# Five places of a hybrid decoder step: three products given later units, output banks in another order, x blocks requested two ahead

## The chip, the cores and the metric

The kernel runs on one core of a Trainium2 chip. The metric is device time in microseconds, the median of several runs. The three runs of the kernel before took 2066.13, 2067.45 and 2067.91 us: median 2067.45.

## The reference

One inference step of one layer (width 2048, float32). A prompt of 1024 tokens with 16 meta tokens ahead of it, and 8 samples of 4 new tokens each with 1024 past tokens in a paged cache, go through the same layer: RMS norm, one input projection into nine parts, a stick-breaking attention branch (8 heads of 128), a gated linear attention branch (GLA, 4 heads or groups with 128 key and 256 value columns), a SiLU gate on each, one output projection, a second RMS norm and the residual. Shortened to what matters:

```python
def branch_inputs(h, w_in, w_alpha, b_alpha):
    u = h @ w_in
    sq, sk, sv, sg, gq, gk, gv, gg, ga = jnp.split(u, idx, axis=-1)
    log_f = jax.nn.log_sigmoid((ga @ w_alpha + b_alpha).astype(jnp.float32)) / GLA_TAU
    ...
def branch_output(o_sb, sg, o_gla, gg, gla_norm_g, w_out):
    o_gla = rms_norm(o_gla, gla_norm_g)
    mixed = jnp.concatenate([o_sb * jax.nn.silu(sg), o_gla * jax.nn.silu(gg)], axis=-1)
    return mixed @ w_out
def stick_break_weights(z, mask):
    sp = jnp.where(mask, jax.nn.softplus(z), 0.0)
    later = lax.cumsum(sp, axis=z.ndim - 1, reverse=True) - sp
    return jnp.where(mask, jnp.exp(jax.nn.log_sigmoid(z) - later), 0.0)
def gla_chunk(S, q, k, v, g):
    b = jnp.cumsum(g, axis=2)
    decay = jnp.where(causal, jnp.exp(jnp.minimum(b_t - b_s, 0.0)), 0.0)
    attn = jnp.einsum('bhtk,bhsk,bhtsk->bhts', q, k, decay)
    o = attn @ v + (q * jnp.exp(b)) @ S
    S_new = jnp.exp(b_last) * S + (k * jnp.exp(b_last - b)).T @ v
    return S_new, o
def reference(...):
    h = rms_norm(x, norm_pre_g)                     # prompt: 16 meta + 1024 tokens; samples: 8 x 4 tokens
    x = x + rms_norm(branch_output(sb(h), sg, gla(h), gg, gla_norm_g, w_out), norm_post_g)
    # also returned: new keys and values, new GLA states, of the prompt and of the 8 samples
```

## The kernel before

**Products.** TensorE computes everything. A float32 matrix is split into a rounded part and a rest, `h` and `l`, and a product is made of three matmuls (h·h, l·h, h·l; L342 to L344 in the input projection, L1593 to L1595 in the output projection). A split is one cast on ScalarE and one subtraction on VectorE. Input projection: 128 output columns at a time (`inproj`), over 16 blocks of the width, with the 1072 tokens in three pieces that have an accumulator each, `acc` (three PSUM banks).

**Weaving.** Everything else is written as generators, and a `Weaver` puts them between the projection's matmuls: after each unit (6 matmuls of one piece, or 12 of an output step) `beat()` runs the generators that are due. `yield n` means: go on n units later. So the numbers behind `yield` set where in TensorE's order a step stands. A scheduler then orders each engine's instructions by priority; `urgent()` raises it. Each engine runs its own order and waits for others by semaphore. All loads and stores go through SyncE's queue (SP) in its order.

**GLA, per group g (four times).** `inside` makes the key tokens and the packed sample keys: `packed` (L921) transposes a block with three copies of the 32 sample tokens (trp_k, L924), copies it on ScalarE (L925) and subtracts on VectorE (L927), which gives a rounded part and a rest in `pk`. `by_token` and `gv_tok` (L935 to L940) transpose keys and values. All of them use one PSUM buffer with the tag "tr". `chunks` then runs over the prompt in eight chunks (U, L1006, and o, L1010 and L1011) and over the eight samples: `km`, `Us` (L1042), the new state `sn` (L1044); the samples' outputs `os` (L1035) are written four at a time, at b = 0 and b = 5. The samples' old states `Sb` have five buffers; a later one is loaded when an earlier one's new state is made.

**Sample attention.** `new_keys` (L1188) makes the sums over the new keys: the product Cs (L1191), copied to `cn` (L1192), and two units later Cn (L1195). `chain(b)` makes the cumulative sums over one sample's past, C (L1219 to L1222), read by VectorE at L1224. Cs, Cn and C share one PSUM buffer with the tag "C".

**Output projection.** The result is cut into quadrants by an algorithm with seven half-size products p, each in steps (p, q) of 4 token tiles t × 8 weight blocks k. The order is (1,0), (2,0), (1,1), (2,1), (6,0), (6,1), (5,0), (3,0), (5,1), (3,1), (7,0), (4,0), (7,1), (4,1). The four accumulators of a q stay in their banks over its one or two products; `take` reads them after each product (L1443 for p = 1 on ScalarE, L1453, L1456, L1461 and L1464 on VectorE), and TensorE can go on with a bank only after it is read. `bank` (L1427) takes banks in turn from six: numbers 0 to 2 are the input projection's, `acc`, and 3 to 5 those of a pool "m". A weight block is loaded (`wr`, 7 buffers), and split into a `ring` of four places (L1394 ScalarE, L1395 VectorE). `form` (L1340, L1343) makes the stationary side, from parts (q, s) loaded back from DRAM.

**The last steps.** `finish0` (L1509) finishes the first 512 tokens during (7,0) to (4,1): for each of 16 blocks n it loads a block of x (`fetch`, L1518, four buffers), forms the residual sum (L1528) and stores it. `load_keep` loads and splits the last step's weights (L1631 to L1635).

## Time and profile before

| | before |
|---|---|
| median of three runs | 2067.45 us |
| the profiled execution | 2066.38 us |
| its span, first to last instruction | 2064.6 us |
| mean granted TensorE clock | 0.999 |
| TensorE busy | 2024.8 us, 98% |
| VectorE / ScalarE / GpSimd busy | 75% / 46% / 4% |
| mean DMA rate | 146 GB/s |

The timeline gives for each instruction its start, its duration, the engine, the line, the operation with output and inputs, and in brackets how long the engine was idle before it and what released it. An "x3" stands for three in a row. The list of waits sums such idle times by line and releaser. The chain of waits goes back from the last instruction to whatever released each step. In the answer by windows a row has the window and its length, the busy time of TensorE's matmuls, its weight loads, VectorE, ScalarE and GpSimd, then the granted clock, the DMA engines' share and GB/s.

### The profile page before, as it was taken

The page shows a single profiled execution, that of the slowest core. Times are in us where ns is not written, and L with a number is a line of the kernel's source. Part 1 is how long each engine was busy: PE and PEld are TensorE (multiplying, and loading weights), DVE is VectorE, ACT ScalarE, POOL GpSimd, SP SyncE. Part 2 cuts the span into 40 slices and gives each one's busy share as a digit, 9 for nine tenths or more (in the row PEclk, how much of TensorE's full clock was granted, in tenths as well). Part 3 has the DMA queues.
Part 4 walks back from the last instruction along what each step waited for, and adds up shares of the span by engine and source line. Part 5 has one row for each costly group of instructions (what it writes and reads, how often), then busy time and mean ns, then how long its engine had stood idle before and what let it go on. Part 6 is the DMA issues. An engine that isn't in the chain of part 4 may idle for free.

```text
span 2064.6 us, 41985 instructions
## 1 busy us (share of the span) xinstructions
PE 2024.8 (98%) x12507; PEld 1863.6 (90%) x12507; DVE 1552.7 (75%) x6282; ACT 953.4 (46%) x2293; POOL 84.6 (4%) x304
## 2 busy tenths in 40 slices
PE   6999999999999999999999999999999999999998
PEld 5999999999999998999999999998888898788776
DVE  7368989888988989899798897978544347454576
ACT  7355555565655656433534335343433325332332
POOL 0012000101000000000000000000000000000000
PEclk9999999999999999999999999999999999999999
DMA  6354454544455442533433433335776666452485
GB/s 202 103 139 148 139 159 133 171 132 147 146 160 146 140 124 76 139 102 82 108 100 79 125 82 110 98 82 155 236 233 231 220 222 200 139 166 74 129 271 202
DMA packets 371821, 301.85 MB, mean 146 GB/s; under 512 B 42360, under 2 KB 312104, under 8 KB 371592
## 3 DMA queue, kind: packets, MB, share of 16 engines
q1 hardware_dynamic: 371288, 298.64, 48.6%
q8 instruction: 98, 1.61, 0.3%
q14 instruction: 131, 1.07, 0.2%
q10 hardware_dynamic: 304, 0.53, 0.1%
HBM read 241.75 MB, written 57.31 MB: 145 GB/s over the span
## 4 chain that ended last, share of the span: by engine, by line
PE 75%; DVE 12%; DMA 6%; ACT 3%; issue 3%; SPq 0%; POOL 0%; DVEq 0%; ACTq 0%; POOLq 0%
PE acc_g L342 5%; PE acc_g L343 5%; PE acc_g L344 5%; DVE jk L464 5%; PE b L1593 4%; PE b L1595 4%; PE b L1594 4%; PE acc_k L342 3%; PE acc_k L344 3%; PE acc_k L343 3%; PE acc_v L342 2%; PE acc_q L342 2%; PE acc_q L344 2%; PE acc_q L343 2%; PE acc_v L344 2%
## 5 line engine op out<-in xcount | busy, mean ns | idle before, releaser
L464 DVE SCALAR_TENSOR_TENSOR jk<-kp,qb 128x128 f32<-128x128 f32 x2048 | 593.8, 290 | 43.5 <-DMA qb<-qsd 1.7
L342 PE MATMUL acc_g<-hT,wh_g 128*128 128x368 f32 (+2 forms) x768 | 251.4, 327 | 0.5 <-DVE ga L389 0.5
L343 PE MATMUL acc_g<-hT,wh_g 128*128 128x368 f32 (+2 forms) x768 | 247.6, 322 | 0.0
L344 PE MATMUL acc_g<-hT,wl_g 128*128 128x368 f32 (+2 forms) x768 | 247.1, 322 | 0.0
L1593 PE MATMUL b<-ring,f 128*128 128x512 f32 x416 | 164.3, 395 | 3.5 <-ACT gx L521 1.4
L464 DVE DVE_READ_ACCUMULATOR jk<-kp,qb 128x1 f32 x2048 | 167.6, 82 | 0.0
L1594 PE MATMUL b<-ring,f 128*128 128x512 f32 x416 | 162.6, 391 | 0.0
L1595 PE MATMUL b<-ring,f 128*128 128x512 f32 x416 | 162.1, 390 | 0.0
L342 PEld LDWEIGHTS acc_g<-hT,wh_g 128*128 128x128 f32 x768 | 144.5, 188 | 13.3 <-issue 10.8
L343 PEld LDWEIGHTS acc_g<-hT,wh_g 128*128 128x128 f32 x768 | 144.6, 188 | 1.1 <-issue 0.4
L1395 DVE TENSOR_TENSOR ring<-wr,ring 128x512 fp32r<-128x512 f32 x104 | 71.3, 689 | 98.4 <-ACT ring L1394 97.7
L344 PEld LDWEIGHTS acc_g<-hT,wl_g 128*128 128x128 f32 x768 | 144.5, 188 | 0.0
L342 PE MATMUL acc_gv<-hT,wh_gv 128*128 128x400 f32 (+2 forms) x384 | 130.5, 340 | 0.0
L1394 ACT CAST ring<-wr 128x512 fp32r<-128x512 f32 x104 | 64.1, 620 | 139.3 <-PE b L1595 77.0
L342 PE MATMUL acc_k<-hT,wh_k 128*128 128x384 f32 (+1 forms) x384 | 126.4, 329 | 0.0
L343 PE MATMUL acc_gv<-hT,wh_gv 128*128 128x400 f32 (+2 forms) x384 | 125.3, 326 | 0.0
L342 PE MATMUL acc_q<-hT,wh_q 128*128 128x368 f32 (+2 forms) x384 | 125.1, 326 | 0.0
L344 PE MATMUL acc_gv<-hT,wl_gv 128*128 128x400 f32 (+2 forms) x384 | 124.8, 325 | 0.0
L344 PE MATMUL acc_k<-hT,wl_k 128*128 128x384 f32 (+1 forms) x384 | 124.7, 325 | 0.0
L343 PE MATMUL acc_k<-hT,wh_k 128*128 128x384 f32 (+1 forms) x384 | 124.5, 324 | 0.0
L344 PE MATMUL acc_q<-hT,wl_q 128*128 128x368 f32 (+2 forms) x384 | 123.4, 321 | 0.0
L343 PE MATMUL acc_q<-hT,wh_q 128*128 128x368 f32 (+2 forms) x384 | 123.4, 321 | 0.0
(454 smaller groups left out, 5294.3 us busy)
## 6 DMA issues: line engine op xcount, KB each, us to landing
kp<-in_cache_k_dram SPq DMA_DIRECT2D x512, 64.0 KB
vr<-in_cache_v_dram SPq DMA_DIRECT2D x64, 512.0 KB
tf<-in_w_out_dram SPq DMA_DIRECT2D x64, 256.0 KB
td<-tf SPq DMA_DIRECT2D x64, 256.0 KB
qb<-qsd SPq DMA_DIRECT2D x64, 256.0 KB
wr_g<-in_w_in_dram SPq DMA_DIRECT2D x64, 256.0 KB
wr<-td SPq DMA_DIRECT2D x56, 256.0 KB
wr<-in_w_out_dram SPq DMA_DIRECT2D x48, 256.0 KB
```

The lines of the kernel that those rows point to most:

```text
L342: mm(acc[c][:, :n], wh, hh[k][:, lo:hi], start=(k == 0), stop=False)
L343: mm(acc[c][:, :n], wh, hl[k][:, lo:hi], start=False, stop=False)
L344: W.mark = mm(acc[c][:, :n], wl, hh[k][:, lo:hi], start=False, stop=(k == NK - 1)).ins
L464: ins = vec.scalar_tensor_tensor(jk[:], kp[:], 1.0, qbs[h, b][:, t, :], ALU.mult, ALU.mult, accum_out=zt[:, t, NPG - 1 - i:NPG - i])
L1394: act.copy(wh, r)
L1395: vec.tensor_tensor(wl, r, wh.bitcast(F32), ALU.subtract)
L1593: mm(bk[:], ah, wh, start=first and k == 0, stop=False, skip_group_check=True)
L1594: mm(bk[:], ah, wl, start=False, stop=False, skip_group_check=True)
L1595: mm(bk[:], al, wh, start=False, stop=last and k == 7, skip_group_check=True)
```

## The change

Five edits. In `inside` the packed sample keys come six units after the last transposed keys and not one. In `chunks` the second four sample outputs come at b = 6 and not 5. In `new_keys` Cs comes after 20 units and not 17. The rotation of output banks starts at 3 and not 0. In `finish0` two x blocks are requested ahead of the first sum and then two ahead of each, and the reads of p = 4's accumulators in `take` (new L1465) become urgent.

```diff
--- before.py
+++ after.py
@@ -909,7 +909,7 @@
             yield 1
             by_token(kt, kd, (8, 1), col, f"k{g}")
             res["kd"], res["ebl"], res["pk"] = kd, ebl, pk
-            yield 1
+            yield 6
             packed(rep_, pk[:], 2, f"k{g}")
 
         def three(src, nm):
@@ -1028,11 +1028,11 @@
                         mm(os_[32 * j:32 * j + 32, i, f * P:(f + 1) * P], at[:48, 8, 16 + NT * b:48 + NT * b],
                            gv[f][:48, 8 * P:9 * P], start=(f == 0 and i == 0), stop=False, skip_group_check=True)
             for b in range(NB):
-                if b in (0, 5):
+                if b in (0, 6):
                     for j in range(4):
-                        e = b // 5 * 4 + j
+                        e = b // 6 * 4 + j
                         n = REAL + NT * e
-                        mm(os_[32 * j:32 * j + 32, b // 5, :], qt[:, n:n + 32], Ss[e][:], start=False, stop=True,
+                        mm(os_[32 * j:32 * j + 32, b // 6, :], qt[:, n:n + 32], Ss[e][:], start=False, stop=True,
                            skip_group_check=True)
                 Sb = Ss[b]
                 km = stg.tile([96, 384], F32R, tag="stg", name=f"km{g}_{b}")[:, :P]
@@ -1186,7 +1186,7 @@
         cn = dp.tile([P, NB, 32], F32, tag="cn", bufs=1, name="cn")
 
         def new_keys():
-            yield 17
+            yield 20
             cps = dps.tile([P, 256], F32, tag="C", name="Cs")
             mm(cps[:], nones[:NSMP, :].bitcast(F32), spb[:].rearrange("p b a -> p (b a)"), start=True, stop=True)
             act.copy(cn[:].rearrange("p b a -> p (b a)"), cps[:])
@@ -1417,7 +1417,7 @@
         pool.memset(ssq, 0.0)
         c11 = [slot(14 + i, f"c11_{i}") for i in range(2)]
         sums_, gains = {}, {}
-        at = itertools.count()
+        at = itertools.count(3)
 
         def gain(b):
             t = op.tile([P, 512], F32, tag="gpost", bufs=2, name=f"gpost{b}_{next(turn)}")
@@ -1461,7 +1461,8 @@
                     vec.tensor_tensor(o, bk[:], o, ALU.add)
                 done(o, 4 + t, 2 + q)
             else:
-                vec.tensor_tensor(u, bk[:], u, ALU.add)
+                with urgent():
+                    vec.tensor_tensor(u, bk[:], u, ALU.add)
                 done(u, 4 + t, q)
 
         def before_last(t):
@@ -1521,8 +1522,9 @@
                 behind_ring(nc.sync.dma_start(xr[i, b], x_prompt[0, 512 + i * P:512 + (i + 1) * P, b * 512:(b + 1) * 512]).ins)
 
             fetch(0)
+            fetch(1)
             for n, (i, b) in enumerate(todo):
-                fetch(n + 1)
+                fetch(n + 2)
                 yield 2 if n < 8 else 1
                 o = sums_[i, b]
                 vec.scalar_tensor_tensor(o, o, r[:, i:i + 1], xs.pop(n), ALU.mult, ALU.add)
```

TensorE in the first group (tr_v is the transpose of the last value block, trp_v and trp_k the packed sample values and keys, U_m the meta chunk). Before:

```order
L342 MATMUL acc_gk_2_17429<-hT_145,wh_gk_0_17432 128x288
L924 MATMUL trp_k_17466<-ident,rep_k_17229 96x128
L343 MATMUL acc_gk_2_17429<-hT_145,wh_gk_0_17432 128x288
L344 MATMUL acc_gk_2_17429<-hT_145,wl_gk_0_17433 128x288
L342 MATMUL acc_gk_2_17429<-hT_146,wh_gk_0_17432 128x288
L343 MATMUL acc_gk_2_17429<-hT_146,wh_gk_0_17432 128x288
L344 MATMUL acc_gk_2_17429<-hT_146,wl_gk_0_17433 128x288
L342 MATMUL acc_gk_0_17427<-hT_147,wh_gk_0_17432 128x400
L935 MATMUL tr_v_1_2_6_17479<-ident,graw_1_2_17358 128x128 x2
L935 MATMUL tr_v_1_2_6_17479<-ident,graw_1_2_17358 48x128
L343 MATMUL acc_gk_0_17427<-hT_147,wh_gk_0_17432 128x400
L344 MATMUL acc_gk_0_17427<-hT_147,wl_gk_0_17433 128x400
```

Now:

```order
L342 MATMUL acc_gk_2_17429<-hT_145,wh_gk_0_17432 128x288
L935 MATMUL tr_v_1_2_6_17475<-ident,graw_1_2_17358 128x128 x2
L935 MATMUL tr_v_1_2_6_17475<-ident,graw_1_2_17358 48x128
L343 MATMUL acc_gk_2_17429<-hT_145,wh_gk_0_17432 128x288
L344 MATMUL acc_gk_2_17429<-hT_145,wl_gk_0_17433 128x288
L342 MATMUL acc_gk_2_17429<-hT_146,wh_gk_0_17432 128x288
L343 MATMUL acc_gk_2_17429<-hT_146,wh_gk_0_17432 128x288
L344 MATMUL acc_gk_2_17429<-hT_146,wl_gk_0_17433 128x288
L924 MATMUL trp_v_1_17506<-ident,rep_v_1_17415 96x128
L342 MATMUL acc_gk_0_17427<-hT_147,wh_gk_0_17432 128x400
L343 MATMUL acc_gk_0_17427<-hT_147,wh_gk_0_17432 128x400
L344 MATMUL acc_gk_0_17427<-hT_147,wl_gk_0_17433 128x400
```

tr_v has taken trp_k's place and trp_v has come up with it; trp_k now stands 22 rows after trp_v, directly ahead of U_0 (L1006). The other groups change in the same way.

TensorE in the last group, at the second sample outputs (os is the output, Sb_n the old state of sample n, Us_n the sample's new outer product). Before:

```order
L344 MATMUL acc_g_1_25012<-hT_151,wl_g_1_25142 128x384
L342 MATMUL acc_g_1_25012<-hT_152,wh_g_1_25141 128x384
L343 MATMUL acc_g_1_25012<-hT_152,wh_g_1_25141 128x384
L1042 MATMUL Us_5_25220<-pv_23246,km_5_25187 128x256
L344 MATMUL acc_g_1_25012<-hT_152,wl_g_1_25142 128x384
L342 MATMUL acc_g_2_25013<-hT_151,wh_g_1_25141 128x304
L343 MATMUL acc_g_2_25013<-hT_151,wh_g_1_25141 128x304
L344 MATMUL acc_g_2_25013<-hT_151,wl_g_1_25142 128x304
L1035 MATMUL os_24902<-Sb_7_25097,gq_22746 32x256
L342 MATMUL acc_g_2_25013<-hT_152,wh_g_1_25141 128x304
L343 MATMUL acc_g_2_25013<-hT_152,wh_g_1_25141 128x304
```

Now:

```order
L1035 MATMUL os_24902<-Sb_6_25057,gq_22746 32x256
L342 MATMUL acc_g_1_25012<-hT_151,wh_g_1_25141 128x384
L343 MATMUL acc_g_1_25012<-hT_151,wh_g_1_25141 128x384
L344 MATMUL acc_g_1_25012<-hT_151,wl_g_1_25142 128x384
L342 MATMUL acc_g_1_25012<-hT_152,wh_g_1_25141 128x384
L343 MATMUL acc_g_1_25012<-hT_152,wh_g_1_25141 128x384
L344 MATMUL acc_g_1_25012<-hT_152,wl_g_1_25142 128x384
L342 MATMUL acc_g_2_25013<-hT_151,wh_g_1_25141 128x304
L1042 MATMUL Us_5_25216<-pv_23246,km_5_25183 128x256
L343 MATMUL acc_g_2_25013<-hT_151,wh_g_1_25141 128x304
L344 MATMUL acc_g_2_25013<-hT_151,wl_g_1_25142 128x304
L1035 MATMUL os_24902<-Sb_7_25097,gq_22746 32x256
```

The products with Sb_4, Sb_5 and Sb_6 stood at rows 8055, 8057 and 8062 of TensorE's order, and stand now at 8068, 8070 and 8071; the one with Sb_7 is row 8082 in both.

VectorE at the end of (4,0) and the start of (7,1) (ring from wr_0 to wr_3 are weight splits of (7,1), wr_7 the last of (4,0); L1528, now L1530, are the residual sums with x blocks xr; u_n the reads of the accumulators, L1464, now L1465). Before:

```order
L1395 TENSOR_TENSOR ring_29184<-wr_7_31285,ring_29183 128x512
L1528 SCALAR_TENSOR_TENSOR y_0_0_30574<-y_0_0_30574,vrt_y_30961,xr_2_31280 128x512
L1635 TENSOR_TENSOR keep_30976<-keep_30976 128x512
L1395 TENSOR_TENSOR ring_29184<-wr_3_31391,ring_29183 128x512
L1528 SCALAR_TENSOR_TENSOR y_1_0_30917<-y_1_0_30917,vrt_y_30961,xr_3_31343 128x512
L1395 TENSOR_TENSOR ring_29184<-wr_0_31323,ring_29183 128x512
L1528 SCALAR_TENSOR_TENSOR y_0_1_30579<-y_0_1_30579,vrt_y_30961,xr_2_31366 128x512
L1395 TENSOR_TENSOR ring_29184<-wr_1_31347,ring_29183 128x512
L1464 TENSOR_TENSOR u_0_29401<-b_0_30937,u_0_29401 128x512
L1464 TENSOR_TENSOR u_1_29403<-b_1_30938,u_1_29403 128x512
L1464 TENSOR_TENSOR u_2_29405<-b_2_30939,u_2_29405 128x512
L1435 TENSOR_TENSOR u_0_29401<-u_0_29401,gpost_93_31143 128x512
```

Now:

```order
L1530 SCALAR_TENSOR_TENSOR y_1_0_30917<-y_1_0_30917,vrt_y_30961,xr_3_31282 128x512
L1395 TENSOR_TENSOR ring_29184<-wr_7_31287,ring_29183 128x512
L1637 TENSOR_TENSOR keep_30978<-keep_30978 128x512
L1395 TENSOR_TENSOR ring_29184<-wr_3_31393,ring_29183 128x512
L1530 SCALAR_TENSOR_TENSOR y_0_1_30579<-y_0_1_30579,vrt_y_30961,xr_2_31345 128x512
L1395 TENSOR_TENSOR ring_29184<-wr_0_31325,ring_29183 128x512
L1530 SCALAR_TENSOR_TENSOR y_1_1_30922<-y_1_1_30922,vrt_y_30961,xr_3_31368 128x512
L1395 TENSOR_TENSOR ring_29184<-wr_1_31349,ring_29183 128x512
L1465 TENSOR_TENSOR u_0_29401<-b_0_30937,u_0_29401 128x512
L1465 TENSOR_TENSOR u_1_29403<-b_1_30938,u_1_29403 128x512
L1465 TENSOR_TENSOR u_2_29405<-b_2_30939,u_2_29405 128x512
L1465 TENSOR_TENSOR u_3_29407<-b_3_30940,u_3_29407 128x512
```

The residual sum y_1_0 with the tenth x block has moved ahead of the split of wr_7, and the sum y_1_1 with the twelfth ahead of ring from wr_1 and of u_0; u_3 follows u_2 at once. In the same way the sum with the seventh block and the split of (4,0)'s second weight now stand ahead of the first read of (7,0)'s accumulators (L1461).

In `new_keys`, Cs moves from row 8270 of TensorE's order to 8288, six matmuls of one unit ahead of the first C, and Cn from before that C to six matmuls behind it.

## The prediction

> **What bounds the kernel now.** I read the page first, then TensorE's waits.
>
> ```profile
> PE 2024.8 (98%) x12507; PEld 1863.6 (90%) x12507; DVE 1552.7 (75%) x6282; ACT 953.4 (46%) x2293; POOL 84.6 (4%) x304
> ...
> PEclk9999999999999999999999999999999999999999
> ```
>
> TensorE is busy for 98% of the span and at full clock in every slice, so the end moves only by what TensorE's own pauses lose or gain. No matmul is added or removed. The list of its waits (us in all, times, longest) has these rows at the places of the change:
>
> ```profile
> PE tr_v L935 <- DVE pk L927: 2.2, 4, 0.6
> ...
> PE Cs L1191 <- issue: 1.5, 1, 1.5
> ...
> PE b L1593 <- ACT gx L521: 1.4, 1, 1.4
> ...
> PE b L1593 <- DVE u L1464: 1.1, 1, 1.1
> ...
> PE b L1593 <- ACT u L1443: 0.9, 1, 0.9
> ...
> PE os L1035 <- DMA Sb<-in_state_gla_dram: 0.6, 1, 0.6
> ```
>
> The edits aim at five of the six: 2.2 + 1.5 + 1.4 + 1.1 + 0.6 = 6.8 us. That is some 0.3% of the run; the work is to say which waits go and which only move. A matmul after a wait also starts more slowly than one in a running sequence; the first rows below show how much. The sum is made against the profiled execution, 2066.38 us (span 2064.6), which lies 1.07 below the median of the runs, 2067.45; the difference is applied to the median. About 0.2%, 4.1 us, is what a measurement of this kernel can tell from no change.
>
> **Packed sample keys (four groups).** The timeline of the first group, ScalarE, VectorE and TensorE rows together:
>
> ```profile
> 978.89 0.48 ACT L940 COPY gv<-tr_v 128x384 f32<-128x384 f32 x1 [0.64 <-PE tr_v L935]
> ...
> 979.42 0.32 PE L924 MATMUL trp_k<-ident,rep_k 128*96 128x128 f32 x1
> ...
> 980.24 0.34 PE L342 MATMUL acc_gk<-hT,wh_gk 128*128 128x400 f32 x1
> ...
> 980.75 0.29 DVE L927 TENSOR_TENSOR pk<-trp_k,pk 32x128 fp32r<-32x128 f32 x1
> ...
> 981.09 0.55 PE L935 MATMUL tr_v<-ident,graw 128*128 128x128 f32 x3 [0.51 <-DVE pk L927]
> ...
> 981.66 0.34 PE L344 MATMUL acc_gk<-hT,wl_gk 128*128 128x400 f32 x1
> ...
> 981.85 0.34 PE L342 MATMUL acc_gk<-hT,wh_gk 128*128 128x400 f32 x1
> ...
> 982.90 0.28 DVE L927 TENSOR_TENSOR pv<-trp_v,pv 32x128 fp32r<-32x128 f32 x1 [0.53 <-ACT pv L925]
> ...
> 985.44 0.61 PE L1006 MATMUL U<-gv,kd 128*128 128x128 f32 x4
> ```
>
> One PSUM buffer serves trp_k, the tr_v behind it and trp_v. tr_v waits until VectorE has read trp_k at 980.75. Normal spacing is 0.19 (981.66 to 981.85), the spacing here (from 980.24) is 0.85: 0.66 lost, of which 0.51 is the listed wait. The other 0.15, the restart, I add to every wait below. Over four groups: 2.2 + 4 × 0.15 = 2.8. In the new order tr_v stands at trp_k's place, and the buffer's reader there is the copy that ends at 979.37, where TensorE arrives at 979.42: no wait. trp_v follows six matmuls after tr_v as before, so nothing changes between these two. trp_k goes to just before U at 985.44, over 2 us after pv's subtract (982.90), so the buffer is free. Its result is not read before the sample chunks, far later; if the buffer were not free, 0.66 would stand at U instead. Term: **−2.8**, bounds −2.9 and −1.4 (half taken back if VectorE, which now does the subtract behind the group's state update, becomes late for the next U).
>
> **Second sample outputs.** VectorE, the DMA issue and TensorE in the last group:
>
> ```profile
> 1408.17 0.48 DVE L1044 SCALAR_TENSOR_TENSOR sn<-Sb,ebl,Us 128x256 f32<-128x256 f32 x1
> ...
> 1408.72 0.46 SPq L993 DMA_DIRECT2D Sb<-in_state_gla_dram  x1
> ...
> 1413.50 0.62 PE L1035 MATMUL os<-Sb,gq 128*32 128x256 f32 x2 [0.61 <-DMA Sb<-in_state_gla_dram]
> ```
>
> The state of sample 7 is loaded into the buffer that sample 2's new state frees at 1408.65, and lands 4.7 us after its issue. In the new order samples 4, 5 and 6 move later, yet the product that waits, sample 7's, stands at the same place, with the same matmuls between it and Us of sample 2. Neither end of this wait moves. In the other groups no such wait is listed, so nothing is to be won there. Term: **0**, bounds −0.8 (wait and restart gone) and +0.2 (the three products now adjacent push the next Us).
>
> **New keys' first product.**
>
> ```profile
> 1445.02 0.41 DVE L1173 TENSOR_TENSOR spb<-spn,bmask 32x256 f32<-32x256 f32 x1
> ...
> 1445.53 0.67 PE L1191 MATMUL Cs<-spb,nones 32*128 32x256 f32 x2 [1.50 <-issue]
> ...
> 1446.13 0.44 PE L342 MATMUL acc_g<-hT,wh_g 128*128 128x368 f32 x1
> ...
> 1446.78 0.70 ACT L1140 CAST dc_h<-ds 128x256 fp32r<-128x256 f32 x1 [0.17 <-DVE ds L1215]
> ...
> 1450.48 0.28 PE L1219 MATMUL C<-ds_h,ntri 128*128 128x256 f32 x1
> ...
> 1451.44 0.41 DVE L1224 TENSOR_TENSOR dz<-dz,C 128x256 f32<-128x256 f32 x1
> ```
>
> The profile says "issue", but Cs starts 0.1 us after spb ends (1445.43): VectorE is the releaser. 1.50 + 0.15 = 1.65 lost. The new place is one unit of 18 matmuls later. From 1446.13 to 1450.48 there are 24 and the small Cn, so at most 0.18 each: without the wait TensorE would be at Cs at 1445.53 − 1.65 = 1443.9, now 18 × 0.175 later, 1447.0, which is 1.6 after spb is ready. What is late next: C of the first sample comes only six matmuls behind Cs and shares its buffer. Cs takes 0.6 (1445.53 to 1446.13), ends about 1447.6, and its copy, now behind dc_h (ends 1447.48) on ScalarE, is done near 1448.0; C arrives at 1447.6 + 6 × 0.175 = 1448.7. Then Cn, now behind C, needs VectorE's read of C (L1224), which ends 1451.85 − 1450.48 = 1.37 after C starts, here 1450.1. Cn arrives after C's four matmuls (some 0.45) and six more: 1450.2. A margin of nothing, so up to 0.5 may be lost. Term: **−1.6**, bounds −1.7 and −1.1.
>
> **Banks in another order.** TensorE rows, then pieces of the chain of waits:
>
> ```profile
> 1726.07 0.39 PE L1595 MATMUL b<-ring,f 128*128 128x512 f32 x1
> ...
> 1727.86 0.50 PE L1593 MATMUL b<-ring,f 128*128 128x512 f32 x1 [1.40 <-ACT gx L521]
> ...
> 1751.91 0.51 PE L1593 MATMUL b<-ring,f 128*128 128x512 f32 x1 [0.94 <-ACT u L1443]
> ```
> ```profile
> 1737.39 5.57 DMA gpost<-in_norm_post_g_dram
> ...
> 1743.02 6.16 DMA q<-md
> ...
> 1749.20 0.70 ACT f L1340 x2
> ...
> 1751.38 0.49 ACT u L1443
> ```
>
> The third output tile needs the bank that ScalarE still empties (gx): 1.40 + 0.15 = 1.55. With the rotation started at three, the first three tiles take other banks and this wait goes. But a step later TensorE waits again, for the copies u that free its accumulators. These stand on ScalarE behind the forms f, which wait for a transfer q issued at 1743.02 and landed at 1749.18. Before q stands another transfer in the chain, not an output product. So TensorE comes 1.55 earlier to 1751.9 and waits 0.94 + 1.55 = 2.5 there. Term: **0**, bounds −1.6 (if the transfers follow TensorE after all) and +0.3 (one ScalarE reordering).
>
> [...] If ScalarE could pass u ahead, the sum would be 1.55 lower.
>
> **x blocks two ahead, and the last reads first.** The chain has the transfer, then VectorE and TensorE rows:
>
> ```profile
> 2000.99 6.39 DMA xr<-in_x_prompt_dram
> ```
> ```profile
> 1982.09 0.75 DVE L1528 SCALAR_TENSOR_TENSOR c<-c,vrt_y,xr 128x512 f32<-128x512 f32 x1 [2.04 <-DMA xr<-in_x_prompt_dram]
> ...
> 1983.98 2.48 DVE L1461 TENSOR_TENSOR y<-b,y 128x512 f32<-128x512 f32 x4
> ...
> 2007.40 0.75 DVE L1528 SCALAR_TENSOR_TENSOR y<-y,vrt_y,xr 128x512 f32<-128x512 f32 x1 [0.62 <-DMA xr<-in_x_prompt_dram]
> ...
> 2008.67 1.88 DVE L1464 TENSOR_TENSOR u<-b,u 128x512 f32<-128x512 f32 x3
> ...
> 2009.41 0.50 PE L1593 MATMUL b<-ring,f 128*128 128x512 f32 x1 [1.15 <-DVE u L1464]
> ```
>
> And the stretch by windows (DMA share and GB/s last):
>
> ```profile
> 1972.00:2012.00 40.00, 38.82 (x189) 30.66 (x182) 27.00 (x45) 14.70 (x34) 0.00 (x0) 1.00 0.89 292
> ```
>
> The 1.15 and the restart make 1.30. u stands on VectorE behind an x block's result (2007.40) and one weight split. Two ahead, each block is asked for sooner, but VectorE's new order spends it: one block more, the twelfth, now stands ahead of u, and its request has about the place on SyncE's queue that the eleventh's had (2000.99). It lands between 2007.4 (same place, same 6.39) and 2006.5 (one block less of backlog: 256 KB at 292 GB/s are 0.9); I take 2006.8, so u starts 0.6 sooner. Another place turns worse: L1461, which frees the banks at 1983.98, now stands behind the seventh block and a weight split. The sixth came at 1982.09, the seventh cannot come less than 0.9 later, its work and the split take 0.75 and 0.6: L1461 starts at 1984.3 to 1985, 0.3 to 1.0 later, and (4,0) with it. I take 0.5. The two do not add, since what TensorE loses at the first it does not wait at the second: 1.30 becomes 0.5 and some 0.3. Term: **−0.5**, bounds −1.3 (both waits gone) and +0.9 (the extra block lands one block's share after 2007.40).
>
> [...]
>
> **Sum.** −2.8 + 0 − 1.6 + 0 − 0.5 = **−4.9**: the profiled execution 2061.5, the median 2067.45 − 4.9 = 2062.5.
>
> **Rivals.**
>
> *All five waits go.* −2.8 − 0.8 − 1.65 − 1.55 − 1.30 = −8.1: 2059.3. For it: each row names its releaser, and each edit is at that spot. Against it: sample 7's row unmoved, and the u wait at 1751.91, which any time won before it runs into. 13%.
>
> *The waits return close behind.* Half the packed term comes back at the next U (1.4), Cn waits 0.5, the x blocks give nothing: −1.4 − 1.1 = −2.5, 2065.0, no difference that can be told. For it: VectorE is 75% busy and every moved read goes into its order. Against it: trp_k's new place has over 2 us of room. 24%.
>
> *Slower: x blocks ahead of the weights.* On VectorE the split of the last weight of (4,0) now stands behind the tenth block; the next weight's request waits for that split's buffer, and the eleventh and twelfth blocks are requested behind it. If the tenth block lands no sooner than one share before the eleventh did, 2006.5, two latencies run in series: its work and the split end at 2007.9, the requests follow by 2008.5, landing 6.39 later at 2014.9, u at 2016.2, 7.5 later than 2008.67. Then −4.4 + 7.5 = +3.1: 2070.6. It decides from a landing of the twelfth block after about 2007.4 + 4.4 = 2011.8. Against it: the tenth block is itself requested one block sooner now, ahead of the weight that it delays. 5%.
>
> **How the numbers follow.** Forecast 58%, rivals 13, 24 and 5%. The forecast's own bounds run from about 2060 to 2064.5, of which a part lies above 2063.3, the limit of faster: of its 58% I count 55 as faster, which with the first rival makes 68%; the middle rival and the other 3 make 27% of no difference; 5% slower (2070.6 itself is still inside 0.2%; worse cases of its kind are not). The range 2059.8 to 2065.8 leaves out about half of the first rival, part of the second and the third.
>
> **What would show it.** After the change: no wait of tr_v for pk in any group; Sb's wait still about 0.6; no wait of Cs, and at most 0.5 at Cn or C; no wait for gx at the start of (1,0), with the wait for u L1443 grown to about 2.5; the u wait at (7,1) about 0.3 to 0.7 with a new one for y L1461 at (4,0). The forecast is wrong if u L1443 does not grow (then 1.5 better), or if new waits of U, Cn or (4,0) exceed 1 us together.

## The result

| | before | after |
|---|---|---|
| median of 11 runs each | 2065.58 us | 2060.44 us |
| lowest to highest | 2062.32 to 2067.91 | 2057.29 to 2062.69 |
| ratio | | 0.9973 (95%: 0.9965 to 0.9981) |
| the profiled execution | 2066.38 | 2062.69 |
| its span | 2064.6 | 2061.0 |

The change makes the kernel faster by 0.27%, some 5.5 us (3.9 to 7.2). The 2062.5 forecast lies two above the median of 2060.44, and this lies inside 2059.8 to 2065.8. Most of these two, 1.9, come from the kernel before: its eleven runs have a median that much below that of the three from which the forecast was counted. The profiled execution of the change was the slowest of its 11; why it was is part of what follows.

TensorE's waits after, at the places of the change (us in all, times, longest):

```profile
PE b L1595 <- DVE u L1465: 2.1, 1, 2.1
PE os L1035 <- DMA Sb<-in_state_gla_dram: 1.5, 1, 1.5
PE b L1595 <- ACT u L1443: 1.5, 1, 1.5
...
PE b L1595 <- DVE y L1461: 1.1, 1, 1.1
```

The rows of tr_v, Cs and gx are gone. The four that stand there add up to 6.2 us, against 7.7 in the six rows before: by the list of waits 1.5 us was won. Yet the span is 3.6 shorter. So this list leaves something out on the winning side, and part of what was won was lost again. Both can be found by setting the start of each matmul beside that of its twin in the profile before. The difference (after minus before) goes down in steps:

| place | step in us | difference behind it |
|---|---|---|
| up to the first packed keys | −0.4 | |
| packed keys, four groups | −0.64, −0.62, −0.65, −0.88: −2.8 | |
| second sample outputs, groups 1 to 3 | −0.73, −0.73, −0.74 | |
| second sample outputs, group 4 | +0.27 | |
| Cs | −1.65 | −6.8 |
| output banks: gx gone, then a weight split (ring L1395) late, then u L1443 longer | −1.73, then +0.53, then +0.55 | −7.5 (from 1752 to 1985) |
| y L1461 at (4,0) | +1.08 | |
| u L1465 at (7,1) | +0.99 | |
| the stretch behind it | +1.75 | −3.7 |

Four rows deserve a look.

**Packed keys.** TensorE in the first group, after:

```profile
977.78 0.34 PE L344 MATMUL acc_gk<-hT,wl_gk 128*128 128x384 f32 x1
...
977.95 0.53 PE L935 MATMUL tr_v<-ident,graw 128*128 128x128 f32 x3
...
984.32 0.27 PE L924 MATMUL trp_k<-ident,rep_k 128*96 128x128 f32 x1
984.43 0.61 PE L1006 MATMUL U<-gv,kd 128*128 128x128 f32 x4
```

tr_v starts 0.17 behind the matmul ahead of it, the normal spacing, and trp_k stands directly ahead of U without a wait. No bracket is left in either row.

**Cs.** After:

```profile
1441.66 0.69 PE L1191 MATMUL Cs<-spb,nones 32*128 32x256 f32 x2
...
1443.40 0.28 PE L1219 MATMUL C<-ds_h,ntri 128*128 128x256 f32 x1
...
1444.99 0.24 PE L1195 MATMUL Cn<-spn,btri 32*32 32x32 f32 x2
```

Nothing waits, neither Cs nor C behind it nor Cn.

**Second sample outputs.** This is the gain that is in no list of waits. The first group before, TensorE's rows around the second four samples (two matmuls a sample):

```profile
1026.98 0.33 PE L344 MATMUL acc_gq<-hT,wl_gq 128*128 128x384 f32 x1
1027.24 0.63 PE L1035 MATMUL os<-Sb,gq 128*32 128x256 f32 x6
1027.81 0.40 PE L342 MATMUL acc_gq<-hT,wh_gq 128*128 128x288 f32 x1
...
1028.83 0.33 PE L342 MATMUL acc_gq<-hT,wh_gq 128*128 128x384 f32 x1
1029.10 0.62 PE L1035 MATMUL os<-Sb,gq 128*32 128x256 f32 x2
1029.65 0.45 PE L343 MATMUL acc_gq<-hT,wh_gq 128*128 128x384 f32 x1
```

and after:

```profile
1027.96 0.34 PE L344 MATMUL acc_gq<-hT,wl_gq 128*128 128x384 f32 x1
1028.22 0.64 PE L1035 MATMUL os<-Sb,gq 128*32 128x256 f32 x8
1028.79 0.45 PE L342 MATMUL acc_gq<-hT,wh_gq 128*128 128x384 f32 x1
```

From the wide matmul ahead to the one behind, six narrow matmuls took 1027.81 − 1026.98 = 0.83, two took 1029.65 − 1028.83 = 0.82, and now eight take 1028.79 − 1027.96 = 0.83. The normal spacing is 0.17. What costs is the visit to these products (32 columns wide, 128*32), about 0.65 each time, and not their number, as long as there are at most four. The trace tells why: the records of the three or four samples last 0.40 each and start only 0.007 apart, so they run side by side (each writes its own 32 rows of `os`), and the two records of one sample start 0.24 apart. More than four do cost more. Elsewhere in the kernel before, in (1,0), eight products of the same shape (`sc`, sixteen records, which start in sets of four) stand between matmuls at 1737.29 and 1738.61:

```profile
1737.61 1.07 PE L1613 MATMUL sc<-wr,small 128*32 128x256 f32 x16
```

That is 1.32 with a normal spacing of 0.23, so 1.09 for two sets of four against 0.65 for one. And an interruption as such costs little: Us, one product of rounded parts with 256 columns, stands between wide ones that start 0.25 apart (1028.45 and 1028.70) where 0.13 is normal.

Before, sample 7's two came in a visit of their own since its state comes last; at b = 6 it is there, and one visit per group is enough.

In the last group there is no such luck, since sample 7's state still comes late. The SyncE issue and TensorE after:

```profile
1403.45 0.45 SPq L993 DMA_DIRECT2D Sb<-in_state_gla_dram  x1
...
1406.34 0.30 PE L344 MATMUL acc_g<-hT,wl_g 128*128 128x304 f32 x1
1408.19 0.62 PE L1035 MATMUL os<-Sb,gq 128*32 128x256 f32 x2 [1.55 <-DMA Sb<-in_state_gla_dram]
```

From issue to product are 4.74 us, as before (1413.50 − 1408.72 = 4.78). Between Us of sample 2 and this product stand two visits now and three before, which lets TensorE arrive earlier, so the wait grows from 0.61 to 1.55.

**The last steps.** VectorE, after:

```profile
1974.98 0.75 DVE L1530 SCALAR_TENSOR_TENSOR c<-c,vrt_y,xr 128x512 f32<-128x512 f32 x1 [3.49 <-DMA xr<-in_x_prompt_dram]
...
1977.56 2.48 DVE L1461 TENSOR_TENSOR y<-b,y 128x512 f32<-128x512 f32 x4
...
2002.10 0.75 DVE L1530 SCALAR_TENSOR_TENSOR y<-y,vrt_y,xr 128x512 f32<-128x512 f32 x1 [1.60 <-DMA xr<-in_x_prompt_dram]
...
2003.37 2.47 DVE L1465 TENSOR_TENSOR u<-b,u 128x512 f32<-128x512 f32 x4
```

and TensorE, with the windows of the same stretch (granted clock, DMA share and GB/s last):

```profile
1978.39 0.47 PE L1595 MATMUL b<-ring,f 128*128 128x512 f32 x1 [1.12 <-DVE y L1461]
...
2004.11 0.51 PE L1595 MATMUL b<-ring,f 128*128 128x512 f32 x1 [2.11 <-DVE u L1465]
...
2006.13 0.63 PE L1595 MATMUL b<-ring,f 128*128 128x512 f32 x1
2006.56 0.63 PE L1596 MATMUL b<-ring,f 128*128 128x512 f32 x1
```
```profile
2001.57:2004.98 3.41, 1.30 (x6) 0.73 (x5) 2.88 (x5) 0.90 (x3) 0.00 (x0) 1.00 1.06 400
2004.98:2008.39 3.41, 3.41 (x10) 2.63 (x9) 3.41 (x7) 2.70 (x8) 0.00 (x0) 0.50 0.90 303
```

The reads that free the banks (L1461, L1465) stand behind sums whose x blocks VectorE waits for, 3.49 and 1.60 us. Both waits of TensorE are longer than before or new. And behind the second, TensorE runs at half clock from 2004.98 to 2008.39: the matmuls come 0.43 apart (2006.13 to 2006.56) where 0.23 is normal.

### The profile page after: what moved, and what is told of

Its sections match the earlier page's. It is cut to its first block, busy times and chain, and to the rows that moved or that the text cites. A ratio compares the mean times of both kernels' runs of the same rounds, so it can differ in the third digit from the quotient of the medians.

```text
span 2061.0 us, 41982 instructions
## 1 busy us (share of the span) xinstructions
PE 2023.1 (98%) x12507; PEld 1864.4 (90%) x12507; DVE 1551.5 (75%) x6282; ACT 953.5 (46%) x2293; POOL 85.1 (4%) x304
## 4 chain that ended last, share of the span: by engine, by line
PE 84%; DVE 7%; DMA 3%; ACT 3%; issue 2%; SPq 1%; POOL 0%; DVEq 0%; ACTq 0%; POOLq 0%
PE acc_g L342 5%; PE acc_g L343 5%; PE acc_g L344 5%; PE b L1595 4%; PE b L1597 4%; PE b L1596 4%; PE acc_gv L342 3%; PE acc_gv L343 3%; PE acc_gv L344 3%; PE acc_k L342 3%; PE acc_k L344 3%; PE acc_k L343 3%; PE acc_v L342 2%; PE acc_v L344 2%; PE acc_v L343 2%; PE acc_q L342 2%
## 5 line engine op out<-in xcount | busy, mean ns | idle before, releaser
L1395 DVE TENSOR_TENSOR ring<-wr,ring 128x512 fp32r<-128x512 f32 x104 | 71.3, 689 | 102.4 <-ACT ring L1394 100.2
```

The lines of the kernel that those rows point to most:

```text
L1395: vec.tensor_tensor(wl, r, wh.bitcast(F32), ALU.subtract)
```

## The experiments

Two theories stand at the start. **T**: the fifth edit loses some 2 us or more, since VectorE's order now holds the bank reads behind late x blocks. Its rival, **H**: it loses nothing by itself; the profiled execution merely came earlier to a wait that is set by transfers, and edits 1 to 4 would have lost as much there. **V**: the second sample outputs gain by saved visits. Its rival, **W** (the prediction's): they change no wait, so they gain nothing. Each experiment was timed against the kernel before on the same chip.

### Edits 1 to 4 without the fifth

The fifth edit is left out:

```diff
             fetch(0)
-            fetch(1)
             for n, (i, b) in enumerate(todo):
-                fetch(n + 2)
+                fetch(n + 1)
...
-                with urgent():
-                    vec.tensor_tensor(u, bk[:], u, ALU.add)
+                vec.tensor_tensor(u, bk[:], u, ALU.add)
```

> The change without its fifth edit (x blocks one ahead, last reads not urgent). Theory T, the fifth edit itself loses 3.8 us of the change's profiled run (1.1 at the first read of (4,0)'s banks, 1.0 more at u, 1.7 by a lower clock behind that wait): this kernel is 7.0 to 7.5 us faster than before, 0.9965 of it, with the wait for u at (7,1) back at about 1.2 and no wait for y L1461. Rival D, the x blocks are paced by the DMA engines, and TensorE, 7 us sooner there, would find them late without the fifth edit too: about as fast as the change, 3.6 to 5.5 us faster than before, with a wait for u of 2 us or more.

2058.82 against 2065.88: ratio 0.9970 (0.9958 to 0.9982). TensorE's waits:

```profile
PE os L1035 <- DMA Sb<-in_state_gla_dram: 1.8, 1, 1.8
PE b L1593 <- ACT u L1443: 1.7, 1, 1.7
...
PE b L1593 <- DVE u L1464: 1.1, 1, 1.1
```

No row of y L1461, and u L1464 as long as in the profile before, although TensorE arrives 8.4 us sooner. The difference to before stays at −8.4 to −8.1 through the last steps, where the change goes from −7.5 to −3.7. T's signs are there and H's, a wait for u of 2 us or more, is not. The median is 1.6 lower than the change's, a difference that the two intervals alone do not tell from none.

### The fifth edit alone

The same two pieces, added to the kernel before.

> The fifth edit alone, on the kernel before. Theory T: slower than before by 2 to 4 us, the waits for y L1461 (1.1) and u (2.1) as in the change, with the lower clock behind u if that wait is over about 2 us. Rival D: the loss needs the time won ahead of it, so this one is within 0.5 us of before, or 0.5 faster as the prediction had it.

2067.79 against 2065.88: ratio 1.0012 (1.0002 to 1.0021), some 2.5 us slower. TensorE's waits:

```profile
PE b L1595 <- DVE u L1465: 2.8, 1, 2.8
```

The loss is at (7,1) alone; y L1461 is not in this list. So the wait at (4,0) does not follow from the edit in every setting; nor does it need the edit, as banks alone shows below. There is no stretch at half clock here, though the pause is longer than the change's 2.1; an estimate of why stands at the end.

### The second sample outputs alone

```diff
-                if b in (0, 5):
+                if b in (0, 6):
                     for j in range(4):
-                        e = b // 5 * 4 + j
+                        e = b // 6 * 4 + j
...
-                        mm(os_[32 * j:32 * j + 32, b // 5, :], qt[:, n:n + 32], Ss[e][:], start=False, stop=True,
+                        mm(os_[32 * j:32 * j + 32, b // 6, :], qt[:, n:n + 32], Ss[e][:], start=False, stop=True,
```

> The second sample outputs alone moved to b = 6. Theory V, each visit of TensorE to the narrow os products costs about 0.65 us whatever their number, and the move makes one visit of two in three groups: 3 x 0.67 = 2.0 us gone there, in the fourth group 0.3 lost (0.85 gone, the wait for the last state 1.0 longer): 1.7 us faster than before. Rival W, only listed waits count: 0 to 0.9 us slower, by the longer wait alone.

2062.19 against 2065.88: ratio 0.9982 (0.9973 to 0.9991), 3.7 us faster (1.9 to 5.6). By the twins, groups 1 to 3 give about 0.7 each, and the whole profile 2.5 to 2.8. V holds and W falls; the size by the medians is above what the visits alone explain, and the lower end of the interval just misses the 1.7 that I worked out.

### Every second output a visit of its own

Each of samples 4 to 7 at its own b, 4 to 7, so that the second half makes four visits in every group:

```diff
-                if b in (0, 5):
-                    for j in range(4):
-                        e = b // 5 * 4 + j
+                if b == 0 or b > 3:
+                    for j in range(4) if b == 0 else (b - 4,):
+                        e = b // 4 * 4 + j
```

> On the kernel before, each of the second four sample outputs at a b of its own (4, 5, 6, 7), so four visits instead of two in the first three groups; the work is the same. Theory V: 2 x 0.65 more in each of three groups, 3.9 us, in the fourth about nothing (three or four visits as before, the wait for the last state shorter by up to 0.6): 3.3 to 3.9 us slower than before, with no new wait listed. Rival W: the same as before or 0.6 faster.

2069.16 against 2065.88: ratio 1.0018 (1.0009 to 1.0028), 3.7 us slower. No matmul was added and no wait of TensorE for a state is left in the list; what it has more of are visits. TensorE's rows around one of them:

```profile
1029.19 0.34 PE L344 MATMUL acc_gq<-hT,wl_gq 128*128 128x384 f32 x1
1029.46 0.62 PE L1035 MATMUL os<-Sb,gq 128*32 128x256 f32 x2
1030.01 0.44 PE L342 MATMUL acc_gq<-hT,wh_gq 128*128 128x384 f32 x1
```

Two products again take 1030.01 − 1029.19 = 0.82. Before had two visits in three groups and four in the last; here are four in each, six more, and 6 × 0.65 = 3.9 is near the 3.7 measured. V holds in both directions.

### The fifth edit in halves

What in the fifth edit loses: the requests two ahead (**F**), or the urgent reads? Edits 1 to 4 with the one, then with the other.

> The change without the urgent reads u, so with x blocks two ahead alone in its fifth edit. Theory F, asking two ahead is what loses, since VectorE's order then puts one x block more ahead of the reads L1461 and u: 3.5 to 5.5 us faster than before, as the change, wait for u 2 to 3 us, that for y L1461 up to 1.1. Rival: the urgent reads lose; then about 7 us faster than before, wait for u about 1.1.

> The change without the x blocks two ahead, with the urgent reads u alone in its fifth edit. Theory F: as without the fifth edit, 6 to 7.5 us faster than before, wait for u about 1.1, none for y L1461. Rival: 3.5 to 5.5 us faster, with the waits of the change.

| beside edits 1 to 4 | median | ratio |
|---|---|---|
| neither | 2058.82 | 0.9970 (0.9958 to 0.9982) |
| requests two ahead | 2060.95 | 0.9978 (0.9969 to 0.9987) |
| urgent reads | 2059.14 | 0.9968 (0.9955 to 0.9980) |
| both: the change, run again | 2060.67 | 0.9974 (0.9965 to 0.9983) |

The order is F's, but the intervals overlap: it is favoured, not shown. In the profiles, the requests two ahead bring back a short wait for y L1461 (0.4) and lose 0.75 in the last steps; with the urgent reads alone there is none for y and u L1465 takes 1.0. That second profile has something else, though. TensorE at (2,0), and a window behind it:

```profile
1745.12 0.50 PE L1594 MATMUL b<-ring,f 128*128 128x512 f32 x1 [2.26 <-ACT u L1443]
```
```profile
1746.00:1748.00 2.00, 2.00 (x7) 1.51 (x6) 2.00 (x5) 1.04 (x3) 0.00 (x0) 0.50 0.97 232
```

Half clock again, behind another long pause, at a place where the change's own profile had a pause of 1.47 and full clock.

### Banks alone

```diff
-        at = itertools.count()
+        at = itertools.count(3)
```

> The output banks in another order alone, on the kernel before. Theory of the prediction: the wait for gx goes (1.4) and the one for u L1443 grows by as much, to about 2.5: no difference, within 0.5 us, or, where the wait of over 2 us brings the lower clock behind it, up to 1.7 slower. Rival: the transfers ahead of u follow TensorE by about half, as in the change's profile (u L1443 at 1.5), 0.6 to 0.9 us faster.

2066.06 against 2066.43: ratio 1.0004 (0.9995 to 1.0013), no difference. TensorE's rows at (2,0):

```profile
1750.42 0.50 PE L1593 MATMUL b<-ring,f 128*128 128x512 f32 x1 [2.00 <-ACT u L1443]
...
1752.40 0.63 PE L1595 MATMUL b<-ring,f 128*128 128x512 f32 x1
1752.83 0.63 PE L1593 MATMUL b<-ring,f 128*128 128x512 f32 x1
```

The gx row is gone, which wins 1.73 by the twins. A late weight split takes 0.46 of it back, the wait for u 1.06, and in this execution the clock behind it costs another 1.6 (0.43 apart at 1752.40). The same list has a row that matters for the fifth edit, which this kernel does not have:

```profile
PE b L1593 <- DVE y L1461: 1.2, 1, 1.2
```

VectorE had waited 3.48 us for the x block ahead of these reads. So a late block at (4,0) can hold TensorE up without the fifth edit.

### Sample 7's state earlier

To edits 1 to 4: sample 7's state goes into a buffer of another pool and is requested after sample 1, not after sample 2; the second outputs come at b = 7.

```diff
-                Ss[b] = gp.tile([P, DV], F32, tag="Sb", bufs=5, name=f"Sb{g}_{b}")
+                if b == 7:
+                    Ss[b] = stage(f"Sb{g}_{b}")[:, :DV]
+                else:
+                    Ss[b] = gp.tile([P, DV], F32, tag="Sb", bufs=5, name=f"Sb{g}_{b}")
...
-                if b in (0, 6):
+                if b in (0, 7):
...
-                if b + 5 < NB:
+                if b + 5 < 7:
                     load_state(b + 5)
+                if b == 1:
+                    load_state(7)
```

> The change without its fifth edit, with the state of sample 7 loaded into another buffer one sample earlier, and the second sample outputs at b = 7. Theory V with a load paced by its buffer: the wait of os for Sb (1.5 in the change, 1.8 without the fifth edit) goes and one visit of 0.65 with it: 2.0 to 2.4 us faster than without the fifth edit, 8.2 to 9.5 us faster than before. Rival: the load is late by the DMA engines and not by its buffer, the wait stays over 1 us, and the time is that without the fifth edit, 6 to 7 us faster than before.

2055.64 against 2065.83: ratio 0.9955 (0.9941 to 0.9969). The wait for Sb is gone and the last group has two visits, with one Us between them. So the load came late because it was requested late, and not by the DMA engines alone. Whether the buffer made it late is not shown, since the edit changes the buffer and the place of the request together, and the rows of the kernel before speak against the buffer:

```profile
1406.20 1.45 SPq L180 DMA_DIRECT2D wr_g<-in_w_in_dram  x1
1406.39 0.48 DVE L1044 SCALAR_TENSOR_TENSOR sn<-Sb,ebl,Us 128x256 f32<-128x256 f32 x1
...
1408.29 0.38 SPq L512 DMA_DIRECT2D md<-gs  x1
```

This sum is sample 2's, whose buffer sample 7 takes, and it ends at 1406.87. The row at 1408.17 in the prediction is sample 3's. The request left at 1408.72, 1.85 after the sum, behind these other transfers on SyncE's queue. The profiled execution again was the slowest of its runs (2059.78), and has the half clock. Its pauses at that place, and the matmuls behind:

```profile
1998.61 0.50 PE L1599 MATMUL b<-ring,f 128*128 128x512 f32 x1 [0.70 <-DVE ring L1400]
...
2001.17 0.58 PE L1598 MATMUL b<-ring,f 128*128 128x512 f32 x1 [1.14 <-DVE u L1469]
2001.55 0.63 PE L1599 MATMUL b<-ring,f 128*128 128x512 f32 x1
```

Two pauses, 0.70 and 1.14, some 2 us apart, were enough here.

### The reads of the accumulators first

Theory **Q**: it is VectorE's order that holds TensorE up; if the late sums stand behind the reads, the wait goes. To edits 1 to 4 with urgent reads: the sums with the eleventh block and later (n > 9) are ordered behind the last read of u (the text before the run says the first).

```diff
-                vec.tensor_tensor(u, bk[:], u, ALU.add)
+                with urgent():
+                    last_u[:] = [vec.tensor_tensor(u, bk[:], u, ALU.add).ins]
...
+                if n > 9 and last_u:
+                    tc.add_manual_dep(sm, last_u[0].name, NOSYNC, reason="behind")
```

> The change without x blocks two ahead, with the reads u urgent and the sums with the eleventh and later x blocks ordered behind the first u on VectorE. Theory Q, u waits only because a late x block stands ahead of it: the wait for u falls from 1.1 to 0.3 or less and the time by about 1 us against the version without the fifth edit, 7 to 8.5 us faster than before. Rival, u is held by the weight splits ahead of it, whose blocks the DMA engines bring late: the wait stays over 0.8 and the time is the same as without the fifth edit.

2058.10 against 2065.83: ratio 0.9965 (0.9953 to 0.9977). The wait for u is gone, and another stands at (4,0) for the same reason, a late sum ahead of the reads:

```profile
PE b L1596 <- DVE y L1461: 1.7, 1, 1.7
```

Q holds for the wait; the gain cannot be told from that of edits 1 to 4.

### All of it

Edits 1 to 4, sample 7's state as above, and on VectorE both groups of reads (L1461 and u) ahead of the sums and of the last weights' splits.

```diff
+                    last_y[:] = [vec.tensor_tensor(o, bk[:], o, ALU.add).ins]
...
+                elif n > 4 and last_y:
+                    tc.add_manual_dep(sm, last_y[0].name, NOSYNC, reason="behind")
...
+                    if last_y:
+                        tc.add_manual_dep(ks, last_y[0].name, NOSYNC, reason="behind")
```

> The change without x blocks two ahead; the state of sample 7 earlier and the second sample outputs at b = 7; on VectorE the sums with the sixth and later x blocks and the splits of the last weights ordered behind the reads L1461 of (7,0), the sums with the eleventh and later ones behind the urgent reads u of (4,0). Theory Q: no wait for Sb, none over 0.4 for y L1461 and u: 10 to 11.5 us faster than before, 0.9947 of it. Rival: the sums put off come back as waits for weight splits later in the step, and the time is that with the earlier state alone, 8 to 9.5 us faster.

2055.83 against 2066.43: ratio 0.9949 (0.9935 to 0.9962), 10.5 us faster (7.9 to 13.4), the fastest kernel of the study by ratio, and its interval lies below that of the change. Of the waits at the places of the change one is left:

```profile
PE b L1603 <- ACT u L1448: 1.0, 1, 1.0
```

None for Sb, y or the u of the last steps. Against the one with only sample 7's state earlier (0.9955) the interval does not tell it apart; its five runs lie from 2053.69 to 2056.26, the other's from 2055.37 to 2059.78.

### The change once more

> The change itself once more, beside the two others on one chip. Theory: 4.5 to 6 us faster than before, waits for y L1461 and u as in its first profile to within 1 us; whether matmuls behind u run at half clock for some 4 us again is open, since a wait of 2.8 had no such stretch behind it in the kernel with the fifth edit alone. Rival, the lower clock follows every wait of 2 us and more: it is there again.

2060.67 against 2066.43: ratio 0.9974 (0.9965 to 0.9983). This profile of the change is 3 us shorter than the first:

```profile
PE b L1595 <- DVE u L1465: 1.5, 1, 1.5
```

There is no row for y L1461, u L1465 takes 1.5 and not 2.1, and the clock is full throughout. The difference to before stays near −7.0 to −6.7. So the loss of the last steps is real on the average (fifth edit alone, 2.5 us) and differs from execution to execution between about 0.3 and 3.8.

## Why the prediction was right or wrong

The direction and the range held. The total was near because two wrong terms nearly cancelled, which was luck. By one of its own signs the forecast stood on the line: it called itself wrong if new waits of U, Cn or (4,0) exceed 1 us together, and the first profile has 1.12 at (4,0), the second none.

| term | predicted | measured |
|---|---|---|
| packed sample keys | −2.8 | −2.8 in the profile |
| second sample outputs | 0 (−0.8 to +0.2) | −1.9 in the profile, −3.7 (−5.6 to −1.9) alone |
| Cs | −1.6 | −1.65 in the profile |
| banks | 0 (−1.6 to +0.3) | −0.65 in the profile; alone +0.8 (−1.0 to +2.7) |
| x blocks and urgent reads | −0.5 (−1.3 to +0.9) | +2.5 (+0.4 to +4.3) alone; +0.3 and +3.8 in two profiles |

**Packed keys: right.** The restart cost of 0.15 on top of each listed wait is borne out: 2.2 is listed, 2.8 was won, 0.62 to 0.65 in three groups and 0.88 in the fourth, against the 0.66 that the spacing gave. trp_k at U found its buffer free. The rival by which half comes back at U did not come.

**Cs: right.** The margin of nothing at Cn held: no wait.

**Second sample outputs: wrong, and the term that I set at nothing.** The step that failed is "neither end of this wait moves. In the other groups no such wait is listed, so nothing is to be won there". The list of waits holds only time in which TensorE stands idle for a releaser. That a separate visit to these narrow products costs 0.65 is in no such list. It was in the trace before, at 1026.98 to 1027.81 and 1028.83 to 1029.65; I read the last group's rows for their bracket and did not take the starts of the wide matmuls ahead and behind. And the sentence "with the same matmuls between it and Us of sample 2" was wrong in the last group: the matmuls are the same, but fewer visits separate them, so TensorE comes earlier and the wait grew to 1.55, where I had put "still about 0.6". The other end was misread as well: by the rows shown under "Sample 7's state earlier", the request waited for its turn on SyncE's queue, and the row at 1408.17 is another sample's.

**Banks: right in substance.** The wait for gx went, and most of it came back. In the change's profile u L1443 reached 1.47, not the 2.5 forecast, a weight split ahead of it cost 0.53, and 0.65 of the gain stayed; alone, u took 2.0, and with the clock nothing stayed. The runs lie on the forecast's value of 0. What I had not priced is the half clock that stood behind that pause of 2.0 and cost another 1.6.

**The fifth edit: wrong in sign.** The step that failed is the choice of 2006.8 for the landing of the block ahead of u, from which followed "u starts 0.6 sooner". Shifted by what TensorE had won until there (2008.67 − 7.5 + 1.1 for the pause at (4,0) = 2002.3), u should have started at 2001.7 by my step; it started at 2003.37, 1.1 later than no change at all. The eleventh and the twelfth block's requests stand 1.85 apart on SyncE's queue and land after VectorE is ready, so the extra sum ahead of u brings a wait of its own (1.60) and its work. At (4,0) the step was right in kind (L1461 behind one block and one split more) and at its upper end in size: 1.08 where I gave 0.3 to 1.0 and took 0.5. But this part is not shown to be the edit's: banks alone has 1.2 there without it, the kernel that puts u's reads first has 1.7 with one block ahead, and the change's second profile has none. The sentence that what is lost at the first place is not waited for at the second failed too: u's wait grew by 0.96, since u stood behind the twelfth block. That block, requested at 1996.40, was used at 2002.10, 5.7 later:

```profile
1994.55 0.86 SPq L1519 DMA_DIRECT2D xr<-in_x_prompt_dram  x1
...
1996.40 0.46 SPq L1519 DMA_DIRECT2D xr<-in_x_prompt_dram  x1
```

**The rivals.** That all five waits go did not come (the rows of Sb and of both u stand in the list). That they return close behind came in part, in the last steps, for which it had "the x blocks give nothing"; they gave less than nothing. The slower one did not come: the twelfth block landed at about 2002.1, ahead of the 2011.8 from which it decides (2004.3 with the 7.5 that had been won by then), but its mechanism, reads behind late x blocks, is the one that made the fifth edit lose.

**What stays open.** Whether the requests or the urgent reads lose more is favoured (the requests) and not shown. So is how much of the wait at (4,0) in the change's first profile is the fifth edit's. And the second sample outputs alone gained 3.7 by the medians, of which three saved visits explain 2.2 (0.73 each by the twins); the rest is unexplained, and the interval reaches down to 1.9.

## What to carry to other kernels

A list of waits prices only idle time: where a few small products interrupt a long run of wide matmuls, take the time from the start of the wide one ahead to that of the one behind, for each kind of product. Where up to four products run side by side, as here, count visits and not products. On an engine that takes its work in order, asking for a transfer earlier can move its consumer ahead of something that others wait for, as on VectorE here (the wait for u at (7,1): 1.15 before, 2.78 with the fifth edit alone); place the reads that free a busy engine's buffers ahead of any work that waits for a transfer. Time won ahead of a wait that follows transfers can come back as a longer wait, as u L1443 shows (0.94 before; 1.5 and 2.0 with the other banks).

## What the runs showed of the hardware

**Up to four narrow products share one price.** Between wide matmuls, one, three and four products of 32 columns by 256 (two, six and eight records, float32) took 0.82, 0.83 and 0.83 us from wide start to wide start; eight took 1.32. Two took 0.56 from their first start to that of the wide one behind (1404.24 to 1404.80 in the change's profile), where one, three and four took 0.55, 0.56 and 0.57. Products of one set of four start 0.007 apart. Whether it is their 32 columns or their unrounded float32 that makes a set dearer than a wide matmul is not shown: Us, with 256 columns too, differs in both.

**Half clock, for 3.41 us at a time.** In four of the twelve profiles of changed kernels the granted clock fell to 0.50 once in the middle of the work and came back by itself. Read in windows of 0.1 us:

| kernel | half clock from | to | idle in the 3.41 us ahead | from this drop to the one after the last matmuls |
|---|---|---|---|---|
| the change, first profile | 2004.98 | 2008.39 | 2.11 | 51.20 us = 15.00 × 3.413 |
| edits 1 to 4 and urgent reads | 1745.51 | 1748.92 | 2.26 | 307.20 us = 90.00 × 3.413 |
| banks alone | 1750.81 | 1754.22 | 2.00 | 310.61 us = 91.00 × 3.413 |
| sample 7's state earlier | 2001.45 | 2004.86 | 1.71 | 51.20 us = 15.00 × 3.413 |

Each lasts 3.41 us and costs half of that, 1.7 (1.75 in the steps above). The clock also falls once TensorE has nothing left to do: its last matmul ended at 2055.06 before and at 2051.37 after, and the clock fell at 2058.86 and at 2056.18. From the drop in the middle to that one are whole numbers of one length, 3.413 us (51.20 / 15), which is that of the stretches themselves. An estimate from these four rows: the clock is set at marks 3.413 us apart that run on through the kernel, whatever the work is. In the 3.41 us ahead of a drop TensorE was idle for 1.71 to 2.26, never throughout.

By this estimate the longest pause of all, 2.78 in the kernel with the fifth edit alone, is cut in two, which may be why no half clock stands behind it. Counted back from its last drop (2060.19) by 15 times 3.413, a mark falls at 2008.99, inside the pause (2007.10 to 2009.88):

```profile
2005.58:2008.99 3.41, 1.52 (x7) 0.94 (x5) 1.12 (x2) 0.00 (x0) 0.00 (x0) 1.00 0.95 320
2008.99:2012.40 3.41, 2.52 (x11) 2.09 (x12) 3.41 (x7) 2.54 (x8) 0.00 (x0) 1.00 1.01 357
```

The mark cuts it into 1.89 and 0.89. But 1.89 between two marks passed here and 1.71 (sample 7's state earlier) did not; what decides between them is not shown. None of the four drops in the middle had less than 1.71 us of idle time ahead of it. Counted by the same marks, from 20 us to the last matmul, the most idle time that passed without a drop was 1.30 in the profile before (1724.35 to 1727.76) and 1.47 in the change's first (1742.15 to 1745.57). Whether a longer pause has a half clock behind it would depend, by the estimate, on where the mark falls, and that differs between two executions of one kernel (2004.98 and 2004.04 near this pause in the two profiles of the change). These two differ in the half clock too: the first, with a pause of 2.11, had it and lost 1.75 in the stretch behind; the second, with 1.50, did not.
